# Residual additions made by accumulating transfers from DRAM instead of a loaded tile and a VectorE add

## The chip, the cores and the metric

The kernel runs on one core of a Trainium2 chip. That core has five engines with queues of their own: TensorE (PE in the profile, its weight loads PEld), VectorE (DVE), ScalarE (ACT), GpSimd (POOL) and SyncE (SP), which here only issues transfers. The metric is the device time of one execution in microseconds (us), lower is better. The median of three runs of the kernel before is 2145.02 us (2145.0 to 2145.69).

## The reference

One step of a two-layer encoder, for a prompt of 1024 rows and a running stream of 32 rows that share the weights. The model dimension is 1024. Cut to what matters:

```python
for i in range(DEPTH):                       # DEPTH = 2
    mod = jax.nn.silu(c) @ w_ada[i] + b_ada[i]
    sh1, sc1, gt1, sh2, sc2, gt2 = jnp.split(mod[:, None, :], N_MOD, axis=-1)
    h = rmsnorm(x, g_norm[i, 0]) * (1 + sc1) + sh1
    if i % N_MIXERS == 0:
        mix, v = sgu_mixer(h, ...)           # gated MLP over chunks of 128 rows
    else:
        mix = pool_mixer(h_ext, ...)         # trailing means of 2, 4, 8, 16 rows
    x = x + gt1 * rmsnorm(mix, g_norm[i, 1])
    h = rmsnorm(x, g_norm[i, 2]) * (1 + sc2) + sh2
    f = jnp.square(jax.nn.relu(h @ ffn_w_up[i])) @ ffn_w_down[i]
    x = x + gt2 * rmsnorm(f, g_norm[i, 3])
```

The two lines `x = x + gt * rmsnorm(...)` are the residual additions that this change is about.

## The kernel before, in words

**Tiles.** Activations stand transposed: 128 partitions times 8 blocks `k` of channels, with rows of the batch along the free dimension. There are three tiles of columns (line 27): 384, 384, and 256 prompt rows plus the 32 rows of the stream, 288 in all. For each tile `t` there is one accumulator `acc[t]` in SBUF (128 x 8 x columns, with 16 columns of halo) in which down products are summed and into which norms and modulation are written in place. Since the accumulator is overwritten, the residual stream `x` itself is kept in DRAM, in `xd[t]`.

**Precision.** Every weight and activation is split into a high part (ScalarE, line 436 and others) and a low part (VectorE, a subtraction recorded at line 80), and three matmuls make one product (lines 946 to 948).

**Stages.** First the adaLN vectors of layer 0 and the gate inputs, then six passes of the sgu mixer (`pu` up, `psp` gating, `po` down), then the feed-forward passes of layer 0 (`pf` up, `pg` down), the pooling mixer of layer 1 (`pp`), the feed-forward of layer 1, and the output. Feed-forward passes are cut by chunk of hidden channels and by tile, ordered so that one tile's norms and mixers run beside another tile's matmuls; in a middle stretch two tiles are combined with sums of columns (`sums_of_columns`, line 1782, whose inputs come over DRAM from `md[t]`).

**Work between the matmuls.** What is not a matmul of the main stream is written as Python generators, *fillers*. `weave` (line 744) is called after each block of products: it takes steps of the weight stream (load, split) and of the fillers as long as a model of the two clocks, `time["pe"]` and `time["dve"]`, says that VectorE has room. A filler that yields True goes on at once, False lets others pass, and a number makes it wait that many modelled us. `finish` forces a filler to its end. The tile framework then sets the order of each engine's queue from this, and places the waits. Each engine runs its own queue strictly in order.

**Buffers.** Up products take 2 banks of PSUM, down products 3 (`ps_dn`, line 159), others 3. Raw weights have 3 buffers (`RAW_SLOTS`), split weights 16. Three small buffers `x3` (`t_x`, line 174) are shared by the loaded residual tiles, the gating inputs, the pooling windows and others.

**The residual.** `residual` (line 852) is used eleven times: after the mixer (`r1`) and after the feed-forward (`r2`), for three tiles in two layers, save the last tile's last one, which ends the kernel in another way. It finishes the norm of `acc[t]` (a matmul with ones gives the sums over channels, `pn`, line 839), then loads `xd[t]` in four pieces of two channel blocks into `x3` buffers (line 859, names `xo`), multiplies each block in place by the gate and the norm (`stt`, line 80 in the profile), adds the loaded piece (`tt`, line 882, recorded at line 80), lets ScalarE square the result and VectorE sum the squares (`Stat.square`, line 788, names `sq_..x`), and stores the new `x` from `acc[t]` to `xd[t]` on SP's queue (line 887). In nine of the eleven the squares follow, for the next norm. In the two of the output (`r2_1`) neither squares nor store follow, but transposes by VectorE (line 2118) and stores of the output, a quarter of which POOL issues (line 2120).

SP issues almost all transfers, weights included, in one queue. POOL issues few: some vectors at the start, memsets for the gating inputs (line 1411) and a quarter of the output stores.

Of the kernel before, what the change touches and what calls it, by code (L numbers as in the profile page):

```python
# [12 lines left out]
ALU = mybir.AluOpType  # L13
AX = mybir.AxisListType

P = 128
# [7 lines left out]
HALO = 16  # L24
# [2 lines left out]
TILES = [(0, 384, 0), (384, 384, 0), (768, 256, DEC)]  # L27
NT = len(TILES)
W_SLOTS = 16
COMBINED = [range(2, 6), range(4, 8)]  # L30
RAW_SLOTS = 3
WINDOWS = (2, 4, 8, 16)
# [3 lines left out]
def tile_stream_encoder_step(  # L36
# [25 lines left out]
    nc = tc.nc  # L62
# [11 lines left out]
    def on_dve(op, fixed, rate):  # L74
        def run(out, *args, **kw):
            n = 1
            for k in out.shape[1:]:
                n *= k
            time["dve"] += fixed + n / rate
            return op(out, *args, **kw)  # L80

        return run

    tt = on_dve(nc.vector.tensor_tensor, 0.16, 930.0)
    stt = on_dve(nc.vector.scalar_tensor_tensor, 0.16, 840.0)
    ts = on_dve(nc.vector.tensor_scalar, 0.1, 930.0)

    def pool(name, **kw):
# [10 lines left out]
    segs = [  # L99
        [(0, p, 0)] + ([(p, s, 1)] if s else []) for _, p, s in TILES  # L100
    ]
# [16 lines left out]
    acc = [const.tile([P, KB, HALO + n], F32, name=f"acc{t}") for t, n in enumerate(ncol)]  # L118
    xd = [dram.tile([P, KB, n], F32, name=f"xd{t}") for t, n in enumerate(ncol)]
# [16 lines left out]
        out=squares, in0=ident[:, 0:DEC], in1=ident[:, DEC : 2 * DEC], op=ALU.add  # L136
    )
    for i in (2, 3):
        nc.vector.tensor_tensor(
            out=squares, in0=squares, in1=ident[:, i * DEC : (i + 1) * DEC], op=ALU.add  # L140
# [7 lines left out]
    def A(t, kb, c0=0, w=None):  # L148
        w = ncol[t] - c0 if w is None else w
        return acc[t][:, kb, HALO + c0 : HALO + c0 + w]  # L150
# [23 lines left out]
    def t_x(name, shape):  # L174
        return small.tile(shape, F32, tag="x3", bufs=3, name=name)
# [28 lines left out]
    coef = small.tile([P, 2, 4, NV, KB], F32, name="coef")  # L204
# [118 lines left out]
    runs = []  # L323
    for l, cs in enumerate(COMBINED):
        before = [[(l, c, [0]) for c in (6, 7)] + [(l, 0, pair), (l, 1, [0]), (l, 1, [1])]]
# [83 lines left out]
    def issue():  # L409
        while state["issued"] < len(stream):  # L410
# [9 lines left out]
            else:  # L420
                r = work.tile([P, 1024], F32, tag="W", bufs=W_SLOTS, name=f"raw{k}")
            if kind == "x":
# [10 lines left out]
    def do_w(key, r):  # L433
        wh = work.tile([P, 1024], F32R, tag="W", bufs=W_SLOTS, name="wh_" + "_".join(map(str, key)))
        wl = work.tile([P, 1024], F32R, tag="W", bufs=W_SLOTS, name="wl_" + "_".join(map(str, key)))
        act(out=wh, in_=r, func=AF.Copy)  # L436
        witem[key] = (wh, wl)
        tt(out=wl, in0=r, in1=wh.bitcast(F32), op=ALU.subtract)
# [3 lines left out]
    def cost(key):  # L442
        return 2 if len(key) != 4 or key[0] != "up" else 4 - key[3]
# [14 lines left out]
    def do_s(key, r):  # L458
        p, i, q = key[1:]
        a, b, sh, sl = (  # L460
            work.tile([P, 1024], F32R, tag="W", bufs=W_SLOTS, name=f"{x}_up_{p}_{i}_{q}")
            if q == 0 or x != "wl"
# [174 lines left out]
    def stream_ready():  # L637
# [3 lines left out]
        if stream[k][0] in "ws":  # L641
# [3 lines left out]
            if i < wtight[0]:  # L645
                return i < W_SLOTS // 2 or worder[i - W_SLOTS // 2] in wdone
            used = sum(cost(key) for key in worder[:i] if key not in wdone)
            return used + cost(worder[i]) <= W_SLOTS - max(
                n for n, first in zip([0] + w_taken, [0] + wtight) if i >= first
# [202 lines left out]
    def residual(st, l, cf, tag, out, store=True, stat=True):  # L852
        t = st.t
        n = ncol[t]
        xos = {}

        def load(k2):
            xos[k2] = t_x(f"xo_{tag}_{k2}", [P, 2, n])
            nc.sync.dma_start(xos[k2], xd[t][:, 2 * k2 : 2 * k2 + 2, :])

        got = []
        yield from st.finish(got)
        r = got[0]
        st2 = Stat(t, tag + "x")
        for half in range(2):
            for k2 in (2 * half, 2 * half + 1):
                load(k2)
            for k2 in (2 * half, 2 * half + 1):
                for k in (2 * k2, 2 * k2 + 1):
                    for c0, w, v in segs[t]:  # L870
                        a = A(t, k, c0, w)
                        stt(
                            out=a,
                            in0=a,
                            scalar=coef[:, l, cf, v, k : k + 1],
                            in1=r[:, c0 : c0 + w],
                            op0=ALU.mult,
                            op1=ALU.mult,
                        )
                    yield True  # L880
                a = acc[t][:, 2 * k2 : 2 * k2 + 2, HALO:]
                tt(out=a, in0=a, in1=xos[k2], op=ALU.add)
                if stat:
                    st2.square(2 * k2, a)
                yield k2 % 2 == 0
        if store:
            nc.sync.dma_start(xd[t], acc[t][:, :, HALO:])
        out.append(st2)
# [399 lines left out]
    for half in range(2):  # L1288
# [3 lines left out]
        ks = slice(4 * half, 4 * half + 4)  # L1292
# [454 lines left out]
    def mix_to_ffn(st, l):  # L1747
        t = st.t
        out = []
        need_ada(l, 2)  # L1750
        yield from residual(st, l, 1, f"r1_{l}_{t}", out)
        if l == 1 and t == NT - 1:
            for q in range(P // DEC):
# [140 lines left out]
    def to_pool(st):  # L1894
# [4 lines left out]
        def run():  # L1899
            need_ada(0, 5)  # L1900
            out = []
            yield from residual(st, 0, 3, f"r2_0_{t}", out)
            need_ada(1, 1)
            got = []
# [152 lines left out]
    def to_out(st):  # L2057
# [48 lines left out]
        def run():  # L2106
            need_ada(1, 5)
            if t == NT - 1:
                yield from last()
                return  # L2110
            yield from residual(st, 1, 3, f"r2_1_{t}", [], store=False, stat=False)
            turned = room("h", t, f"turned{t}")
            dst = y_prompt[0, col0 : col0 + npr, :].rearrange(
                "(b i) (k q c) -> q k i b c", i=DEC, q=P // DEC, c=DEC
            )
            for k in range(KB):
                time["dve"] += 0.1 + npr / 930.0
                nc.vector.transpose(out=turned[:, k, :], in_=A(t, k))
                for q in range(P // DEC):
                    (nc.gpsimd if q == 3 else nc.sync).dma_start(  # L2120
                        dst[q, k],
                        turned[DEC * q : DEC * (q + 1), k, :].rearrange("p (b c) -> p b c", c=DEC),
                    )
                yield 5.0
# [50 lines left out]
```

## Time and profile before

| | |
|---|---|
| median of three runs | 2145.02 us |
| the profiled execution | 2145.2 us |
| its span, first to last instruction | 2143.4 us |
| TensorE busy | 2120.2 us (99%) |
| VectorE busy | 1533.1 us (72%) |
| ScalarE busy | 1011.7 us (47%) |
| POOL busy | 15.3 us (1%) |
| mean granted TensorE clock | 0.999 |
| moved by transfers | 321.88 MB, mean 150 GB/s |

The profile is of one execution. Busy time of TensorE includes matmuls that overlap; the groups of instructions give a mean duration per matmul of about 0.32 us, while one starts every 0.17 us. A row of waits tells which engine and line stood idle, and whose end released it. A helper hides the line: nearly all VectorE operations are recorded at line 80, so tiles tell them apart. Landing is the time from a transfer's issue to the semaphore that tells of its end.

### The profile page before, as it was taken

The numbers are of one execution on the slowest core, as the hardware profiler recorded it, in microseconds if no ns is written. First come the engines' busy times: TensorE is split into PE (matmuls) and PEld (weight loads), VectorE is DVE, ScalarE is ACT, GpSimd is POOL, SyncE is SP. The second block draws the span as 40 slices with busy tenths as digits, with TensorE's granted clock in tenths as the row PEclk, the third lists the DMA queues.
The fourth block names the chain that finished last, engine by engine and source line by source line (L and its number), as shares of the span: only waits on it lengthen the run. The fifth ranks groups of instructions, "written<-read, shape, count | busy, mean of one in ns | idle before, by whom it ended". The sixth has DMA issues, their size and how long they took to land.

```text
span 2143.4 us, 33175 instructions
## 1 busy us (share of the span) xinstructions
PE 2120.2 (99%) x13041; PEld 2043.8 (95%) x13041; DVE 1533.1 (72%) x2786; ACT 1011.7 (47%) x1772; POOL 15.3 (1%) x34
## 2 busy tenths in 40 slices
PE   9999999999999999999999999999999999999998
PEld 6778999999999999999999999999999999999998
DVE  6787747466878668897778778969578654578464
ACT  5534322233456255244545556665355443365454
POOL 0000000000000000000000000000000000001000
PEclk9999999999999999999999999999999999999999
DMA  8487524353537454343434576665265322158662
GB/s 309 147 264 211 167 85 128 93 156 103 171 98 239 129 157 131 109 128 118 157 110 132 162 213 201 194 189 169 85 192 156 99 70 59 55 160 232 149 202 77
DMA packets 366002, 321.88 MB, mean 150 GB/s; under 512 B 39731, under 2 KB 328027, under 8 KB 365845
## 3 DMA queue, kind: packets, MB, share of 16 engines
q1 hardware_dynamic: 365172, 318.87, 48.8%
q8 instruction: 102, 1.67, 0.3%
q0 software_dynamic: 640, 0.88, 0.1%
q14 instruction: 56, 0.45, 0.1%
q10 hardware_dynamic: 32, 0.01, 0.0%
HBM read 279.22 MB, written 40.49 MB: 149 GB/s over the span
## 4 chain that ended last, share of the span: by engine, by line
PE 87%; DVE 5%; DMA 5%; ACT 2%; issue 1%; SPq 0%; DVEq 0%; ACTq 0%
PE pg L947 10%; PE pg L946 10%; PE pg L948 10%; PE pf L946 6%; PE pf L947 6%; PE pf L948 6%; PE pf_0a L1610 3%; PE po L947 3%; PE po L946 3%; PE po L948 3%; PE pu L946 3%; PE pu L948 3%; PE pu L947 3%; PE pv L974 2%; PE pv L973 2%; PE pv L975 2%
## 5 line engine op out<-in xcount | busy, mean ns | idle before, releaser
L946 PE MATMUL pg<-fh,wh_dn 128*128 128x384 f32 (+1 forms) x1344 | 431.6, 322 | 1.3 <-ACT fh L1359 1.1
L947 PE MATMUL pg<-fl,wh_dn 128*128 128x384 f32 (+1 forms) x1344 | 428.5, 319 | 0.9 <-DVE fl L80 0.9
L948 PE MATMUL pg<-fh,wl_dn 128*128 128x384 f32 (+1 forms) x1344 | 428.2, 319 | 0.0
L946 PE MATMUL pf<-hh,wh_up 128*128 128x288 f32 (+1 forms) x1024 | 323.2, 316 | 3.8 <-ACT wh_up L436 2.6
L947 PE MATMUL pf<-hl,wh_up 128*128 128x288 f32 (+1 forms) x1024 | 321.9, 315 | 0.8 <-DVE hl L80 0.8
L948 PE MATMUL pf<-hh,wl_up 128*128 128x288 f32 (+1 forms) x1024 | 322.1, 315 | 0.0
L946 PEld LDWEIGHTS pg<-fh,wh_dn 128*128 128x128 f32 x1344 | 252.1, 188 | 5.0 <-ACT fh L1359 3.4
L947 PEld LDWEIGHTS pg<-fl,wh_dn 128*128 128x128 f32 x1344 | 252.2, 188 | 2.2 <-DVE fl L80 1.1
L948 PEld LDWEIGHTS pg<-fh,wl_dn 128*128 128x128 f32 x1344 | 252.2, 188 | 0.0
L80 DVE TENSOR_TENSOR acc<-acc,pg 128x384 f32<-128x384 f32 (+1 forms) x336 | 172.4, 517 | 86.2 <-PE pg L948 85.3
L80 DVE TENSOR_TENSOR wl_dn<-raw,wh_dn 128x1024 fp32r<-128x1024 f32 x144 | 175.8, 1221 | 64.9 <-ACT wh_dn L436 60.3
L80 DVE TENSOR_TENSOR wl_up<-raw,wh_up 128x1024 fp32r<-128x1024 f32 (+1 forms) x160 | 160.3, 1008 | 77.6 <-ACT wh_up L436 66.3
L80 DVE SCALAR_TENSOR_TENSOR aa<-raw,csil,aa 128x512 f32<-128x512 f32 (+1 forms) x364 | 205.8, 624 | 11.6 <-DMA raw<-in_w_ada_dram 11.5
L436 ACT ACTIVATE wh_dn<-raw 128x1024 fp32r<-128x1024 f32 x144 | 151.4, 1055 | 96.8 <-PE pg L947 48.3
L946 PEld LDWEIGHTS pf<-hh,wh_up 128*128 128x128 f32 x1024 | 192.0, 188 | 5.0 <-ACT wh_up L436 3.1
L947 PEld LDWEIGHTS pf<-hl,wh_up 128*128 128x128 f32 x1024 | 192.2, 188 | 1.3 <-DVE hl L80 1.0
L948 PEld LDWEIGHTS pf<-hh,wl_up 128*128 128x128 f32 x1024 | 192.5, 188 | 0.3 <-DVE wl_up L80 0.2
L436 ACT ACTIVATE wh_up<-raw 128x1024 fp32r<-128x1024 f32 x112 | 118.3, 1058 | 134.9 <-PE pf L947 80.3
L946 PE MATMUL pu<-hh,wh_u 128*128 128x384 f32 (+1 forms) x384 | 125.8, 328 | 0.0
L946 PE MATMUL po<-ush,wh_o 128*128 128x384 f32 (+1 forms) x384 | 123.6, 322 | 0.0
L948 PE MATMUL pu<-hh,wl_u 128*128 128x384 f32 (+1 forms) x384 | 123.4, 321 | 0.0
L947 PE MATMUL pu<-hl,wh_u 128*128 128x384 f32 (+1 forms) x384 | 123.3, 321 | 0.0
(453 smaller groups left out, 4130.5 us busy)
## 6 DMA issues: line engine op xcount, KB each, us to landing
raw<-in_ffn_w_up_dram SPq DMA_DIRECT2D x144, 512.0 KB, 4.4
raw<-in_ffn_w_down_dram SPq DMA_DIRECT2D x144, 512.0 KB, 3.6
raw<-in_w_ada_dram SPq DMA_DIRECT2D x96, 512.0 KB, 4.7
raw<-in_sgu_w_in_dram SPq DMA_DIRECT2D x40, 512.0 KB, 4.2
xd<-acc SPq DMA_DIRECT2D x8, 1536.0 KB, 7.6
raw<-in_sgu_w_out_dram SPq DMA_DIRECT2D x24, 512.0 KB, 3.9
xo_r<-xd SPq DMA_DIRECT2D x32, 384.0 KB, 3.4
vd<-vt SPq DMA_DIRECT2D x32, 256.0 KB, 4.4
```

Source lines behind the costliest of these rows:

```text
L80: return op(out, *args, **kw)
L436: act(out=wh, in_=r, func=AF.Copy)
L946: mm(ps[:, :n], wh, rh, start=i == 0, stop=False)
L947: mm(ps[:, :n], wh, rl, start=False, stop=False)
L948: mm(ps[:, :n], wl, rh, start=False, stop=i == last)
L973: mm(ps[:m, :], a_h, wh[:, o : o + 512], start=k == 0, stop=False)
L974: mm(ps[:m, :], a_h, wl[:, o : o + 512], start=False, stop=False)
L975: mm(ps[:m, :], a_l, wh[:, o : o + 512], start=False, stop=k == KB - 1)
L1610: mm(ps[:, :n], u, v, start=first and k == 0 and x == 0, stop=k == 3 and x == 2, skip_group_check=True,)
```

## The change

The load of `xd[t]` into a tile and the VectorE addition are taken out. Instead all blocks of a half are scaled, and then two transfers, issued by POOL, add `xd[t]` from DRAM onto `acc[t]` in SBUF (`accum_op`). The squares are no longer taken block by block behind each addition, but after all four transfers, behind a modelled wait of `ADDED` = 4.0 us. The store of the new `x` on SP's queue follows the squares in the program.

```diff
+ADDED = 4.0
...
     def residual(st, l, cf, tag, out, store=True, stat=True):
         t = st.t
         n = ncol[t]
-        xos = {}
-
-        def load(k2):
-            xos[k2] = t_x(f"xo_{tag}_{k2}", [P, 2, n])
-            nc.sync.dma_start(xos[k2], xd[t][:, 2 * k2 : 2 * k2 + 2, :])
-
         got = []
         yield from st.finish(got)
         r = got[0]
         st2 = Stat(t, tag + "x")
         for half in range(2):
-            for k2 in (2 * half, 2 * half + 1):
-                load(k2)
-            for k2 in (2 * half, 2 * half + 1):
-                for k in (2 * k2, 2 * k2 + 1):
-                    for c0, w, v in segs[t]:
-                        a = A(t, k, c0, w)
-                        stt(
-                            out=a,
-                            in0=a,
-                            scalar=coef[:, l, cf, v, k : k + 1],
-                            in1=r[:, c0 : c0 + w],
-                            op0=ALU.mult,
-                            op1=ALU.mult,
-                        )
-                    yield True
-                a = acc[t][:, 2 * k2 : 2 * k2 + 2, HALO:]
-                tt(out=a, in0=a, in1=xos[k2], op=ALU.add)
-                if stat:
-                    st2.square(2 * k2, a)
-                yield k2 % 2 == 0
+            for k in range(4 * half, 4 * half + 4):
+                for c0, w, v in segs[t]:
+                    a = A(t, k, c0, w)
+                    stt(
+                        out=a,
+                        in0=a,
+                        scalar=coef[:, l, cf, v, k : k + 1],
+                        in1=r[:, c0 : c0 + w],
+                        op0=ALU.mult,
+                        op1=ALU.mult,
+                    )
+                yield k % 2 == 0
+            for k in (4 * half, 4 * half + 2):
+                ks = slice(k, k + 2)
+                nc.gpsimd.dma_start(
+                    out=acc[t][:, ks, HALO:], in_=xd[t][:, ks, :], accum_op=ALU.add
+                )
+        if stat:
+            yield ADDED
+            for k2 in range(4):
+                st2.square(2 * k2, acc[t][:, 2 * k2 : 2 * k2 + 2, HALO:])
                 yield k2 % 2 == 0
         if store:
             nc.sync.dma_start(xd[t], acc[t][:, :, HALO:])
```

Because the modelled VectorE time and the dependencies change, the order of several queues changes with it. Lines of the changed kernel are one higher near the top and three lower below the edit. Three places follow; the numbers at the ends of names count buffers.

VectorE's queue in the first residual of tile 0 (`r1_0_0`), before. `acc0` with `coef` is a scaling, `xo` the addition, `sq` a sum of squares, `po` the accumulation of another tile's down products:

```order
L80 TENSOR_SCALAR acc0_72<-acc0_72,coef_123,r_rs_0_5007 128x384 x3
L80 TENSOR_TENSOR acc0_72<-acc0_72,xo_r1_0_0_0_5054 128x2x384
L80 TENSOR_TENSOR acc1_73<-acc1_73,po4_1_1_5078 128x384
L80 TENSOR_SCALAR acc0_72<-acc0_72,coef_123,r_rs_0_5007 128x384
L80 TENSOR_TENSOR acc1_73<-acc1_73,po4_1_2_5095 128x384
L80 TENSOR_TENSOR acc0_72<-acc0_72,xo_r1_0_0_1_5056 128x2x384
L80 TENSOR_SCALAR acc0_72<-acc0_72,coef_123,r_rs_0_5007 128x384 x2
L80 TENSOR_TENSOR acc1_73<-acc1_73,po4_1_3_5115 128x384
L80 TENSOR_TENSOR acc0_72<-acc0_72,xo_r1_0_0_2_5109 128x2x384
L80 TENSOR_TENSOR sq_r1_0_0x_5075<-sq_r1_0_0x_5075 128x768
```

The same place in the changed kernel:

```order
L81 TENSOR_SCALAR acc0_72<-acc0_72,coef_123,r_rs_0_5007 128x384 x4
L81 TENSOR_TENSOR acc1_73<-acc1_73,po4_1_1_5072 128x384
L81 TENSOR_SCALAR acc0_72<-acc0_72,coef_123,r_rs_0_5007 128x384 x3
L81 TENSOR_TENSOR acc1_73<-acc1_73,po4_1_2_5091 128x384
L81 TENSOR_SCALAR acc0_72<-acc0_72,coef_123,r_rs_0_5007 128x384
L81 TENSOR_TENSOR acc1_73<-acc1_73,po4_1_3_5108 128x384
L81 TENSOR_TENSOR sq_r1_0_0x_5136<-sq_r1_0_0x_5136 128x768
L81 TENSOR_TENSOR acc1_73<-acc1_73,po4_1_4_5122 128x384
L81 TENSOR_TENSOR sq_r1_0_0x_5136<-sq_r1_0_0x_5136 128x768
L81 TENSOR_TENSOR acc1_73<-acc1_73,po4_1_5_5149 128x384
L81 TENSOR_TENSOR sq_r1_0_0x_5136<-sq_r1_0_0x_5136 128x768
```

The additions are gone, the scalings close up, and the sums of squares follow the last scaling with one or two accumulations between.

SP's queue where the last tile's residual of layer 1 ends, before (`raw` are weight loads, `md2<-acc2` the store from which the sums of columns begin, `acc2<-md` and `sums_m` their loads):

```order
L428 DMA raw346_15737<-in_ffn_w_up_dram 128x8x128
L428 DMA raw347_15782<-in_ffn_w_down_dram 128x4x256
L428 DMA raw348_15826<-in_ffn_w_down_dram 128x4x256
L1823 DMA sums_m0_15905<-md1_80 128x384
L1823 DMA sums_m1_15989<-md1_80 128x384
L1774 DMA md2_81<-acc2_74 1024x1x288
L428 DMA raw349_15872<-in_ffn_w_down_dram 128x4x256
L428 DMA raw350_15927<-in_ffn_w_down_dram 128x4x256
L1819 DMA acc2_74<-md1_80 128x384
```

And in the changed kernel:

```order
L429 DMA raw342_15472<-in_ffn_w_down_dram 128x4x256
L429 DMA raw343_15518<-in_ffn_w_up_dram 128x8x128
L1820 DMA sums_m0_15557<-md1_80 128x384
L1820 DMA sums_m1_15641<-md1_80 128x384
L1771 DMA md2_81<-acc2_74 1024x1x288
L429 DMA raw344_15579<-in_ffn_w_up_dram 128x8x128
L429 DMA raw345_15625<-in_ffn_w_up_dram 128x8x128
L1816 DMA acc2_74<-md1_80 128x384
```

The store moved from behind weight load 348 to behind weight load 343, five loads earlier.

POOL's queue from the gating of the fifth group on, before:

```order
L1411 MEMSET vl4_2_5010 128x256
L1411 MEMSET vl5_2_5256 128x256
L1411 MEMSET vl6_2_5708 128x256
L1411 MEMSET vl7_2_5939 128x256
L2120 DMA out_0_dram<-turned0_19127 32x12x32 x8
```

And in the changed kernel:

```order
L1408 MEMSET vl4_2_5010 128x256
L1408 MEMSET vl5_2_5256 128x256
L875 DMA acc0_72<-xd0_75 128x2x384 x4
L1408 MEMSET vl6_2_5700 128x256
L1408 MEMSET vl7_2_5931 128x256
L875 DMA acc1_73<-xd1_76 128x2x384 x4
L875 DMA acc2_74<-xd2_77 128x2x288 x4
```

Four transfers stand in POOL's queue for each residual, the first four ahead of the last two memsets.

## The prediction

> **What bounds the kernel now.** I read the page's first part, then TensorE's waits, then the stretches in which the eleven residual additions run, then the transfers.
>
> ```profile
> span 2143.4 us, 33175 instructions
> ...
> PE 2120.2 (99%) x13041; PEld 2043.8 (95%) x13041; DVE 1533.1 (72%) x2786; ACT 1011.7 (47%) x1772; POOL 15.3 (1%) x34
> ```
>
> The span holds 2120.2 us of busy TensorE, so 23.2 us is all that anything outside TensorE could give. Not all of it is near the change; the waits say who ends the idle time:
>
> ```profile
> PE pf L946 <- ACT wh_up L436: 2.6, 2, 2.0
> PE pv L974 <- DVE wl_v L80: 1.7, 1, 1.7
> PE pn_rf L839 <- ACT sc_rf L824: 1.5, 1, 1.5
> ...
> PE pg L947 <- DVE fl L80: 0.9, 1, 0.9
> ...
> PE pf L947 <- DVE hl L80: 0.8, 1, 0.8
> ```
>
> No row names the residual addition or its loaded tile. Next, the residual stretches (columns: stretch, length, then busy time of PE, PEld, DVE, ACT, POOL with counts, granted clock, DMA share, GB/s), first narrow, then wider ones:
>
> ```profile
> 1200.00:1226.00 26.00, 26.00 (x199) 26.00 (x198) 25.08 (x39) 16.14 (x26) 0.00 (x0) 1.00 0.66 207
> 1318.00:1343.00 25.00, 25.00 (x191) 25.00 (x190) 24.60 (x38) 16.01 (x24) 0.00 (x0) 1.00 0.69 211
> ```
>
> ```profile
> 1195.00:1270.00 75.00, 72.24 (x530) 71.05 (x530) 64.39 (x98) 43.15 (x71) 0.00 (x0) 1.00 0.67 207
> ...
> 1550.00:1630.00 80.00, 78.98 (x453) 78.09 (x452) 58.03 (x108) 45.75 (x78) 0.00 (x0) 1.00 0.62 188
> 1915.00:1980.00 65.00, 62.69 (x457) 62.11 (x456) 60.91 (x106) 36.14 (x62) 9.95 (x16) 1.00 0.78 211
> ```
>
> Inside a residual VectorE is nearly full (25.08 of 26.00 us), yet TensorE never stops there. It stops a little later: 75.00 - 72.24 = 2.76 us in 1195 to 1270, 1.02 us in 1550 to 1630, 2.31 us in 1915 to 1980. The whole prize near the change is thus about 6 us, 0.3% of the time, and any loss must come from new waits.
>
> **What is removed.**
>
> ```profile
> L859 SPq DMA_DIRECT2D xo_r<-xd x44: 319/339/2374, 512.6 to 1959.3; - x44
> L80 DVE TENSOR_TENSOR acc<-acc,xo_r x44: 751/952/968, 530.7 to 1966.6; 128x768 f32<-128x768 f32 x32, 128x576 f32<-128x576 f32 x12
> ```
>
> 44 additions leave VectorE: 32 x 0.952 + 12 x 0.751 = 39.5 us of its 1533.1. None of it is on TensorE's path by itself; it counts where VectorE's backlog later holds TensorE up. There is one clear such place, after the second residual of layer 1's first tile:
>
> ```profile
> L80 DVE TENSOR_TENSOR acc<-acc,xo_r 128x768 f32<-128x768 f32 x4 | 3.8, 952 | 0.0
> ```
>
> ```profile
> 1239.82 1.23 DVE sums L566
> 1241.07 5.38 DMA raw<-in_ffn_w_up_dram
> 1246.47 1.07 ACT wh_up L436
> ...
> 1261.65 1.07 ACT wh_up L436
> 1262.76 0.40 PE pf L946
> ```
>
> The first row is VectorE's work in 1195 to 1270, the second view the chain there (start, length, what). VectorE ends its adaLN sums late, which frees a raw buffer late, so a weight load starts late and TensorE waits for wh_up: the 2.6 us above. Four additions, 3.8 us, stand ahead of those sums. If VectorE ran 3.8 us earlier all 2.6 us would go; if it spends the saving waiting for squares, nothing goes. Bounds 0 and -2.6; I take the middle, **-1.3**, because the new waits fall on the same queue.
>
> Second place: the wait of 0.9 us for fl. Its chain:
>
> ```profile
> 1594.99 5.79 DMA md<-acc
> ...
> 1623.60 0.56 DVE fl L80
> 1624.21 0.44 PE pg L947
> ```
>
> It starts at the store md<-acc that ends the last tile's residual of layer 1. In the changed order this store stands five weight loads earlier in SP's queue (shown ahead of this section). Bounds 0 and -0.9; I take **-0.9**. The waits of 1.5 and 0.8 us lie in 1915 to 1980, where the additions (the last starts at 1966.6) mostly follow them: 0, with -1.5 as the bound.
>
> SP loses 44 issues. It does wait in them, but far longer for the weights' raw buffers:
>
> ```profile
> SPq L428 <- DVE wl_dn L80: 372.5, 110, 12.9
> ...
> SPq L859 <- DVE acc L80: 46.3, 18, 9.6
> ```
>
> A raw buffer freed by VectorE, not SP's place in line, dates the weight loads. I cost this at 0 beside the 2.6 us already counted. In return the store of the residual on SP now waits for the fourth landing instead of an addition, with weight loads queued behind it; three raw buffers in flight and the converted weights cover that as long as it is a few us.
>
> **What is added.** 44 transfers issued by POOL, and behind them ScalarE's squares, then VectorE's sums of squares, both in order with work for TensorE. The trace shows no accumulating transfer; the nearest rows are these:
>
> ```profile
> xd<-acc SPq DMA_DIRECT2D x8, 1536.0 KB, 7.6
> ...
> xo_r<-xd SPq DMA_DIRECT2D x32, 384.0 KB, 3.4
> ```
>
> ```profile
> L2120 POOL DMA_DIRECT2D out_dram<-turned x16: 615/617/653, 1942.6 to 1976.5; - x16
> ```
>
> POOL's own time is 44 x 0.617 = 27 us on an engine busy 15.3 us: nothing waits for that in itself. One memset of the gating stands behind the first four issues in POOL's queue; before, it waited for the third addition of that same residual, so it comes hardly later. Landing: a plain load of the same bytes lands 3.4 us after a 0.339 us issue, so from POOL 3.4 + 0.617 - 0.339 = 3.7 us. From 384 to 1536 KB landing grows by 4.2 us, so 1.4 us for each further 384 KB and 2.0 us fixed. If the addition makes the engines handle every byte twice, one takes 2.0 + 0.3 + 2.8 = 5.1 us, and four in a row need 2.8 us each.
>
> How long may it take? In the changed order the eighth scaling stands ahead of VectorE's fourth po accumulation and the sum that needs the fourth square behind the sixth: two blocks of twelve matmuls.
>
> ```profile
> 837.05 2.08 PE pf_0b L1610 x12
> ```
>
> ```profile
> L794 ACT ACTIVATE sq_r_0x<-acc x12: 827/847/850, 531.7 to 1221.6; 128x768 f32<-128x768 f32 x12
> ```
>
> ```profile
> L80 DVE TENSOR_TENSOR acc<-acc,pg 128x384 f32<-128x384 f32 (+1 forms) x336 | 172.4, 517 | 86.2 <-PE pg L948 85.3
> ```
>
> Two blocks are 4.2 us; less the square of 0.85 the landing may take 3.3 us before ScalarE and VectorE stand still. TensorE stops later still: of three banks for down products it can fill two more, 2 x 2.08 less the 0.52 us accumulation = 3.6 us. So:
> - landing of 3.7 us: 0.4 us late, covered: 0 lost;
> - every byte twice: issues for a whole residual spread over about 4.2 us, the fourth lands 5.1 + 3 x 2.8 = 13.5 us after the first issue, 9.3 us after its own, 6.0 us late: 2.4 us lost.
>
> Nine residuals take squares (the two of the output do not; their transposes follow directly, and there VectorE waits as long at most). Ends: 0 and 9 x 2.4 = 22 us. The 384 KB load is the nearest row, since bytes, layout and direction are the same, so I stay near the low end, 0.5 us each, **+4.5**: the transfer engines are already 0.66 to 0.69 busy there with weights; against that, three of the nine residuals are a quarter smaller (128x576). If that cover is gone (lateness above 3.6 us) each us more costs nine.
>
> How the engines treat an addition decides between the ends. The Trainium skill, page "Collectives: The Full Stack", section "The bandwidth ceiling: the fold count and why AG ≠ RS ≠ AR", says that an adding transfer is slowed by its two source reads and not by the add, 62.28 against 32.35 GB/s. By it the sum would use the second case, +22 in place of +4.5; no row here has such a transfer, so nothing tests it yet.
>
> **Sum.** -1.3 - 0.9 + 4.5 = +2.3 us. The profiled execution took 2145.2 us (span 2143.4 and 1.8 around it), 0.2 above the runs' median of 2145.02: 2145.2 + 2.3 - 0.2 = **2147.3 us**. A measurement of this kernel tells about 0.2% from no change, 4.3 us, so this is no change.
>
> **Rivals.**
> - *The landings hold up ScalarE and VectorE* (slower). Place: squares of the nine residuals. Price: up to 2.4 us each, 2145.0 - 2.2 + 22 = 2165 us; it decides from 0.75 us each (4.3 + 2.2 over nine), a fourth landing some 7.7 us after its issue. For it: DMA share 0.66 to 0.69 in the stretches and a byte handled twice, the mechanism to which the page's rule leads. Against: the store row, which moves four times the bytes in 7.6 us; and VectorE gets 3.8 us back in each residual to spend on waiting.
> - *VectorE's relief shows, landings stay hidden* (faster). Then the waits of 2.6, 0.9 and 1.5 us go: 2145.0 - 5.0 = 2140 us. For it: VectorE is full in every residual stretch, and the change empties it just there. Against: those waits also hang on loads of 4 to 5 us, and all three must go to pass 4.3 us.
> - That the additions are not moved at all cannot be: the order has no xo tile left and four POOL transfers per residual.
>
> **Chances.** Forecast (2141 to 2149.3) 0.48, slower rival 0.35, faster rival 0.17. The range 2140 to 2162 leaves out about 0.08 of the faster and 0.10 of the slower rival.
>
> **What would show it.** Right: no acc<-acc,xo_r rows, VectorE busy near 1533.1 - 39.5 = 1494 us; POOL-issued transfers landing in 4 to 6 us; idle time of the squares ended by the DMA, some us per residual, but TensorE's own waits still under 30 us in all and no new row above 2 us; the waits for wh_up and fl smaller. Wrong: landings of 8 us or more, TensorE waiting for fh, acc or wh_up beside each residual (slower), or all three old waits gone with no new one (faster). What I could miss most is queueing: weights and four adding transfers at once on engines two thirds busy.

## The result, and the profile after

The changed kernel takes 2311.15 us (median; 2306.5 to 2313.5) beside 2145.36 us of the kernel before on the same chip: a ratio of 1.077, 95% interval 1.0751 to 1.0789. The change costs 166 us. The forecast was 2147.3 us and no change. It was wrong: even its slower rival was priced at 2165 us.

The profiled execution took 2312.9 us. From its page, the span and the busy times:

```profile
span 2311.1 us, 33201 instructions
...
PE 2158.9 (93%) x13041; PEld 2071.3 (90%) x13041; DVE 1503.7 (65%) x2742; ACT 1012.3 (44%) x1772; POOL 68.7 (3%) x78
```

VectorE lost the additions as intended: 2786 - 2742 = 44 instructions and 29.4 us of busy time (39.5 were forecast; the removed durations do add up to that, but the records of neighbouring operations overlap, and busy time counts an overlap once). TensorE idles 2311.1 - 2158.9 = 152.2 us, where it idled 23.2 before: 129.0 us more. The same 13041 matmuls are also busy 2158.9 - 2120.2 = 38.7 us longer. Together that is the 167.7 us between the two spans. The second part goes with the granted clock, whose mean fell from 0.999 to 0.968.

The stretches with TensorE's busy time, clock, DMA share and GB/s place the loss. First a stretch of the kernel before, in which TensorE never stops:

```profile
500.00:730.00 230.00, 230.00 (x1454) 1.00 0.52 159
```

Then the changed kernel. Its first and third stretch hold residuals, the second holds none:

```profile
500.00:730.00 230.00, 196.62 (x1196) 0.92 0.49 131
730.00:1130.00 400.00, 397.13 (x2287) 1.00 0.41 127
1130.00:1430.00 300.00, 254.51 (x1651) 0.92 0.54 148
```

TensorE's waits name the engines that ScalarE's squares and VectorE's sums block:

```profile
PE pf L943 <- ACT r L1531: 51.7, 9, 13.1
PE pg L943 <- ACT fh L1356: 25.5, 7, 9.4
PE pf L945 <- DVE wl_up L81: 17.1, 2, 15.4
PE pn_r_0x L840 <- ACT sc_r_0x L825: 10.5, 1, 10.5
```

The cause is one view further down. These are the 44 transfers themselves: the duration of an issue on POOL, what ended POOL's idle time ahead of one, who waited, and the landing:

```profile
L875 POOL DMA_DIRECT2D acc<-xd x44: 1189/1207/1261, 530.7 to 2121.3; - x44
...
  issue: 218.5, 25
...
  ACT sq_r_0x L795: 57.9, 12
  ACT sq_r_2x L795: 53.2, 11
  ACT sq_r_1x L795: 47.1, 12
...
DMA to landing us min/median/max: 4.6/5.5/8.2
```

An issue takes 1.207 us, and 25 times POOL stands idle ahead of one with nothing that the profile shows to wait for ("issue"). One of these waits, 102.4 us ahead of the first transfer of a residual, is only the time between two residuals; the other 24 are 116.1 us, 3.9 to 7.3 us each. In order of time, the first residual on POOL and ScalarE (start, length, idle time before and its releaser):

```profile
530.70 1.26 POOL L875 DMA_DIRECT2D acc<-xd  x1 [17.61 <-DVE acc L81]
536.47 1.23 POOL L875 DMA_DIRECT2D acc<-xd  x1 [4.51 <-issue]
541.98 1.21 POOL L875 DMA_DIRECT2D acc<-xd  x1 [4.28 <-issue]
547.73 1.21 POOL L875 DMA_DIRECT2D acc<-xd  x1 [4.54 <-issue]
```

```profile
536.29 0.85 ACT L795 ACTIVATE sq_r_0x<-acc 128x768 f32<-128x768 f32 x1 [7.59 <-DMA acc<-xd]
...
553.42 0.84 ACT L795 ACTIVATE sq_r_0x<-acc 128x768 f32<-128x768 f32 x1 [5.15 <-DMA acc<-xd]
```

Each transfer is issued only when the one before has landed: the first square starts at 536.29, POOL's next issue at 536.47. The fourth piece lands 22.7 us after the first issue (553.42 - 530.70). In the kernel before, the fourth square of this residual started at 540.14:

```profile
531.70 0.85 ACT L794 ACTIVATE sq_r_0x<-acc 128x768 f32<-128x768 f32 x1 [3.12 <-DVE acc L80]
...
540.14 0.85 ACT L794 ACTIVATE sq_r_0x<-acc 128x768 f32<-128x768 f32 x1 [2.88 <-DVE acc L80]
```

One residual thus ends 13.3 us later, and there are eleven, nine of them with squares.

### The profile page after: what moved, and what is told of

Same layout as the page of the kernel before. It is cut to its first block, busy times and chain, and to the rows that moved or that the text cites. A ratio compares the mean times of both kernels' runs of the same rounds, so it can differ in the third digit from the quotient of the medians.

```text
span 2311.1 us, 33201 instructions
## 1 busy us (share of the span) xinstructions
PE 2158.9 (93%) x13041; PEld 2071.3 (90%) x13041; DVE 1503.7 (65%) x2742; ACT 1012.3 (44%) x1772; POOL 68.7 (3%) x78
## 3 DMA queue, kind: packets, MB, share of 16 engines
q0 software_dynamic: 12608, 17.01, 5.0%
## 5 line engine op out<-in xcount | busy, mean ns | idle before, releaser
L943 PE MATMUL pg<-fh,wh_dn 128*128 128x384 f32 (+1 forms) x1344 | 438.9, 327 | 38.5 <-ACT fh L1356 25.5
L944 PE MATMUL pg<-fl,wh_dn 128*128 128x384 f32 (+1 forms) x1344 | 435.6, 324 | 6.0 <-DVE fl L81 5.8
L945 PE MATMUL pg<-fh,wl_dn 128*128 128x384 f32 (+1 forms) x1344 | 433.7, 323 | 0.0
L943 PE MATMUL pf<-hh,wh_up 128*128 128x288 f32 (+1 forms) x1024 | 328.5, 321 | 53.9 <-ACT r L1531 51.7
L945 PE MATMUL pf<-hh,wl_up 128*128 128x288 f32 (+1 forms) x1024 | 327.1, 320 | 17.1 <-DVE wl_up L81 17.1
L943 PEld LDWEIGHTS pg<-fh,wh_dn 128*128 128x128 f32 x1344 | 256.9, 191 | 45.2 <-ACT fh L1356 28.6
L944 PEld LDWEIGHTS pg<-fl,wh_dn 128*128 128x128 f32 x1344 | 257.2, 191 | 10.2 <-DVE fl L81 8.9
L945 PEld LDWEIGHTS pg<-fh,wl_dn 128*128 128x128 f32 x1344 | 257.2, 191 | 0.2 <-DVE wl_dn L81 0.2
L944 PE MATMUL po<-usl,wh_o 128*128 128x384 f32 (+1 forms) x384 | 124.0, 323 | 0.0
L945 PE MATMUL po<-ush,wl_o 128*128 128x384 f32 (+1 forms) x384 | 123.9, 323 | 0.0
```

Source lines behind the costliest of these rows:

```text
L943: mm(ps[:, :n], wh, rh, start=i == 0, stop=False)
L944: mm(ps[:, :n], wh, rl, start=False, stop=False)
L945: mm(ps[:, :n], wl, rh, start=False, stop=i == last)
```

## The experiments

The program has no wait between the transfers, so there are two explanations of the single file. *Room*: a transfer under way takes up part of a memory for descriptors (the entries that say which pieces to move), whose size the kernel sets (`dynamic_dma_scratch_size`, 1024 bytes a partition here), and that holds one such transfer. *One at a time*: accumulating transfers follow one another whatever the memory. All times are medians, each beside the kernel before in the same session (2147.74, 2148.42 and 2145.91 us in the three sessions; where that matters, a difference between sessions is taken from the ratios).

**A little more room.**

```diff
-        "TRN2", target_bir_lowering=False, num_devices=1, dynamic_dma_scratch_size=1024
+        "TRN2", target_bir_lowering=False, num_devices=1, dynamic_dma_scratch_size=1088
```

> The changed kernel with one number changed: the memory kept in SBUF for the descriptors of POOL's transfers is 1088 bytes a partition instead of 1024. Theory 1, room: POOL issues the next accumulating transfer only when the memory for the descriptors has room, and 1024 bytes hold one transfer of 384 KB but not two; if the small step is enough for a second one, the issues come in pairs 1.2 us apart (now 5.5 to 5.8 us apart), the fourth lands some 12 to 14 us after the first issue instead of 22 to 23, and the time falls to 2200 to 2260 us; if it is not enough, nothing changes, which leaves theory 1 open. Theory 2, one at a time: accumulating transfers follow one another whatever the memory, spacing 5.5 to 5.8 us, time 2305 to 2315 us.

Measured: 2244.01 us, ratio 1.0456 (1.0439 to 1.0474). POOL in the first residual, then ScalarE's fourth square there:

```profile
533.03 2.52 POOL L875 DMA_DIRECT2D acc<-xd  x2 [17.61 <-DVE acc L81]
538.54 1.21 POOL L875 DMA_DIRECT2D acc<-xd  x1 [2.99 <-issue]
541.41 1.21 POOL L875 DMA_DIRECT2D acc<-xd  x1 [1.66 <-issue]
```

```profile
547.07 0.84 ACT L795 ACTIVATE sq_r_0x<-acc 128x768 f32<-128x768 f32 x1 [2.19 <-DMA acc<-xd]
```

Two are now issued back to back, the third when the first has landed, and the fourth piece is there 14.0 us after the first issue. 64 bytes a partition are worth 67 us. *One at a time* falls, and that the number of bytes changes the spacing is what *room* says. Two transfers do not fit in 1024 bytes and do in 1088, so if they take equal shares, one takes more than 512 and at most 544 bytes a partition.

**Room for all four.** The bytes are paid for by one raw weight slot, so a control has two slots and the old memory.

```diff
-RAW_SLOTS = 3
+RAW_SLOTS = 2
...
-        "TRN2", target_bir_lowering=False, num_devices=1, dynamic_dma_scratch_size=1024
+        "TRN2", target_bir_lowering=False, num_devices=1, dynamic_dma_scratch_size=4096
```

> The changed kernel with 4096 bytes a partition for the descriptors of POOL's transfers, paid for by one raw weight slot less (two instead of three). Theory 1, room: all four transfers of a residual are issued about 1.2 us apart; each then lands in 5.5 us or somewhat more since they share the engines, the fourth 9 to 13 us after the first issue; the residuals' part of the loss falls by more than half, time 2170 to 2220 us plus whatever the missing raw slot costs. Theory 2, one at a time: spacing stays 5.5 to 5.8 us and the time is 2311 us or more.

The control, without the last line:

> The changed kernel with two raw weight slots instead of three and the descriptor memory as it was (1024 bytes): the control for the run with 4096 bytes, 2263.8 us. If the larger descriptor memory alone did what that run showed, this one is slower than it by about what four transfers at once are worth, 70 to 110 us: 2330 to 2375 us. If the missing slot had nothing to do with the rest, it is near 2311 us, and the larger memory is worth some 47 us.

Measured: 2263.81 us (ratio 1.0534) with room, 2360.17 us (1.0981) in the control. With room, POOL and ScalarE in the first residual:

```profile
545.27 3.77 POOL L875 DMA_DIRECT2D acc<-xd  x3 [17.60 <-DVE acc L81]
549.37 1.19 POOL L875 DMA_DIRECT2D acc<-xd  x1 [0.33 <-DVE acc L81]
```

```profile
550.49 0.85 ACT L795 ACTIVATE sq_r_0x<-acc 128x768 f32<-128x768 f32 x1 [7.22 <-DMA acc<-xd]
553.17 0.85 ACT L795 ACTIVATE sq_r_0x<-acc 128x768 f32<-128x768 f32 x1 [1.83 <-DMA acc<-xd]
555.64 0.85 ACT L795 ACTIVATE sq_r_0x<-acc 128x768 f32<-128x768 f32 x1 [1.62 <-DMA acc<-xd]
557.75 0.84 ACT L795 ACTIVATE sq_r_0x<-acc 128x768 f32<-128x768 f32 x1 [1.26 <-DMA acc<-xd]
```

POOL waits for room no longer, and the memory alone is worth 96 us beside the control, as *room* expected (70 to 110). The missing slot costs 1.0981 - 1.0770 in the ratios, 45 us; with it the expected 2170 to 2220 becomes 2215 to 2265 us, which just holds the measured time. Without it the four transfers at once would leave some 70 us of the loss (an estimate: 1.0534 less 0.0211). What is left is the landings: with all four under way they come 2.7, 2.5 and 2.1 us apart, the fourth 12.5 us after the first issue.

**Half as large, twice as many.**

```diff
-            for k in (4 * half, 4 * half + 2):
-                ks = slice(k, k + 2)
+            for k in range(4 * half, 4 * half + 4):
+                ks = slice(k, k + 1)
```

> The changed kernel with eight transfers of one block (192 KB) for a residual instead of four of two blocks. Theory 1, room: half as many descriptors each, so that at least two are under way together: issues about 1.2 us apart in pairs or more, the eighth lands no later than the fourth did, 16 to 23 us after the first issue, and the first block of all lands earlier; time 2250 to 2310 us. Theory 2, one at a time: eight landings of some 4 to 5 us follow one another, 32 to 40 us for a residual, and the time rises to 2380 to 2480 us.

Measured: 2247.55 us, 64 us better than four larger ones, with the same bytes and the old memory, and a little better than expected from *room*. The issue of half the rows takes 875 ns instead of 1207:

```profile
L875 POOL DMA_DIRECT2D acc<-xd x88: 856/875/1582, 529.8 to 2056.9; - x88
...
  issue: 23.0, 18
```

POOL's waits without a shown cause fell from 116.1 us (without the one between residuals) to 23.0 us.

**The same transfer without the addition.**

```diff
-            nc.sync.dma_start(xos[k2], xd[t][:, 2 * k2 : 2 * k2 + 2, :])
+            nc.gpsimd.dma_start(xos[k2], xd[t][:, 2 * k2 : 2 * k2 + 2, :])
```

> The kernel before with one word changed: the four loads of x of each residual are issued by POOL instead of SP, plain copies into a tile, and VectorE adds as before. It tells the price of POOL's issue from that of the accumulation. If what costs is any transfer of 384 KB from POOL's queue, the issues are 4 to 6 us apart here too and the time is 2200 us or more. If it is the accumulation, the loads are issued about 1.2 us apart, land in 3.4 to 4.5 us, hidden behind the DVE work as SP's are, and the time is 2140 to 2155 us.

Measured: 2146.19 us, ratio 0.9997 (0.9987 to 1.0006). Plain loads from POOL:

```profile
L859 POOL DMA_DIRECT2D xo_r<-xd x44: 538/538/585, 513.4 to 1963.5; - x44
...
DMA to landing us min/median/max: 3.0/3.6/6.9
```

POOL's queue is not the cost; the accumulating transfer is. For the same bytes its issue takes 1207 instead of 538 ns and its landing 5.5 instead of 3.6 us. Two things differ, the addition and the destination: `acc` has 16 columns of halo between its blocks, the tile `xo` has no gaps (the run with a spare tile, below, separates them). The packets of POOL's queue (packets, MB, share) suggest why the memory fills; the rows are of the kernel before, this run, the changed kernel and the run with half-size transfers:

```profile
q0 software_dynamic: 640, 0.88, 0.1%
```

```profile
q0 software_dynamic: 4160, 17.01, 2.8%
```

```profile
q0 software_dynamic: 12608, 17.01, 5.0%
```

```profile
q0 software_dynamic: 13312, 17.01, 5.0%
```

A plain transfer makes (4160 - 640)/44 = 80 packets, an accumulating one (12608 - 640)/44 = 272, half of one (13312 - 640)/88 = 144. If room goes by packets, 513 to 544 bytes for 272 are 1.9 to 2.0 bytes each (an estimate), and of the half-size transfers three fit into 1024 bytes and a fourth does not. In the first residual of that run three are issued back to back from 529.83 to 532.57, and the fourth, whose block was scaled by 531.1, only at 534.05.

**Nothing added at all.** Two runs price VectorE's relief, one in the new order and one in the old.

```diff
-            for k in (4 * half, 4 * half + 2):
-                ks = slice(k, k + 2)
-                nc.gpsimd.dma_start(
-                    out=acc[t][:, ks, HALO:], in_=xd[t][:, ks, :], accum_op=ALU.add
-                )
```

> The changed kernel with the 44 accumulating transfers left out: x is not added at all, so the sums are not the reference's; everything else, the order of the squares included, stays. Theory 1, the transfers are the loss: ScalarE's squares wait for nothing long, the loss goes, and the time is 2135 to 2150 us; the distance to 2147.7 is all that the removed VectorE additions and loads are worth. Theory 2, the new order is the loss (all squares of a tile after all its products, in one block at the end): the time stays above 2170 us.

```diff
-            for k2 in (2 * half, 2 * half + 1):
-                load(k2)
...
-                tt(out=a, in0=a, in1=xos[k2], op=ALU.add)
```

> The kernel before with the 44 additions and their 44 loads left out, all else in its old order; x is not added, so the result is another. It prices the relief that the prediction put at 2.2 us. If the predicted gain terms are right: 2145 to 2147 us beside 2148 us of the kernel before, ratio 0.998 to 0.9995. If VectorE's relief is worth the full stalls near the residuals: 2141 to 2143 us. If it is worth nothing: within 0.05% of the kernel before, and the 2151.6 us of the new order without transfers then show a price of the order.

Measured: 2151.64 us in the new order, ratio 1.0013 (1.0004 to 1.0022); 2148.25 us in the old, ratio 1.0016 (1.0007 to 1.0025). Both are slower than any gain that was expected: with no addition at all the kernel is not faster. They lie 3.2 and 2.3 us above the kernel before, with intervals that overlap, so the new order by itself costs next to nothing, and taking the additions and their loads away is worth nothing here. Why is seen in the old-order run at the place where the prediction had booked its largest gain:

```profile
PE pf L945 <- DVE wl_up L80: 2.4, 1, 2.4
```

The 2.6 us of waiting for wh_up were two waits, the longer of 2.0 us; here stands one of 2.4 us for wl_up, with 0.5 us of others. The clock in the same place (stretch, length, TensorE busy, clock, DMA share, GB/s), first in the kernel before, then in this run:

```profile
1262.00:1264.00 2.00, 1.24 (x9) 1.00 0.62 183
1264.00:1266.00 2.00, 2.00 (x17) 1.00 0.76 203
```

```profile
1264.00:1266.00 2.00, 0.11 (x1) 1.00 0.46 112
1266.00:1268.00 2.00, 1.45 (x6) 0.60 0.60 174
1268.00:1270.00 2.00, 2.00 (x11) 0.55 0.97 268
```

Before, the clock stayed at 1.00 through the pause, of which the end is shown. Here it fell, and for some 4 us TensorE did 11 matmuls in 2 us instead of 17.

**Transfers for which nobody waits.**

```diff
-                nc.gpsimd.dma_start(
-                    out=acc[t][:, ks, HALO:], in_=xd[t][:, ks, :], accum_op=ALU.add
-                )
+                e = t_x(f"e_{tag}_{k}", [P, 2, n])
+                nc.gpsimd.memset(e, 0.0)
+                nc.gpsimd.dma_start(out=e, in_=xd[t][:, ks, :], accum_op=ALU.add)
```

> The changed kernel, its transfers still accumulating and its descriptor memory still 1024 bytes, but adding x onto a spare tile that POOL has cleared and nobody reads; x is so left out of the result. POOL's issues, the 44 serial landings and their traffic stay, and only the waits of the squares, the transposes and the store for a landing go. Theory 1, waiting for landings is the whole loss: 2148 to 2156 us, as with the transfers left out (2151.6 us), with POOL's spacing still 5 to 6 us. Theory 2, the transfers disturb others by themselves (weights arrive later, engines slower): a good part of the 160 us stays, over 2180 us.

Measured: 2178.41 us, between the two expectations: by the ratios, 133 us below the changed kernel and 30 above the run without transfers. The 30 us come at least in part from the edit: its spare tiles are buffers that other loads use too, and SP and TensorE stand at those:

```profile
SPq L1909 <- DMA e_r<-xd: 24.4, 1, 24.4
```

```profile
PE pp L2026 <- DMA wg<-in_pool_w_grp_dram: 14.0, 1, 14.0
```

The spare tile has no gaps, and its transfers are lighter (issue, then packets, then landing):

```profile
L877 POOL DMA_DIRECT2D e_r<-xd x44: 857/872/1249, 513.1 to 1929.5; - x44
```

```profile
q0 software_dynamic: 6976, 17.01, 4.7%
```

```profile
e_r<-xd POOLq DMA_DIRECT2D x32, 384.0 KB, 5.4
```

That is (6976 - 640)/44 = 144 packets. So the addition alone, onto a tile without gaps like the plain load's, raises 80 packets to 144, 538 ns to 872 and a landing of 3.6 us to 5.4. The gaps of `acc` raise the packets further to 272 and the issue to 1207 ns, and leave the landing at 5.5 us. (No run makes a plain load into a tile with gaps.)

The edit thus changes more than the waits: half the packets, and issues that no longer wait for scalings (the first at 513.1 instead of 530.7). Their spacing is set by the memsets ahead of them, which wait for an earlier transfer (104.6 us in 28 waits), and at times two are issued together. About 133 of the 166 us go with the waits for landings and with these differences; of the other 33 this run cannot tell how much is the transfers' own traffic.

**Squares held back.** What remains once two fit (96 us in the run with 1088 bytes) could be squares that stand too early in ScalarE's queue.

```diff
-ADDED = 4.0
+ADDED = 12.0
...
-        "TRN2", target_bir_lowering=False, num_devices=1, dynamic_dma_scratch_size=1024
+        "TRN2", target_bir_lowering=False, num_devices=1, dynamic_dma_scratch_size=1088
```

> The run with 1088 bytes for descriptors, and ADDED 12.0 instead of 4.0, so that the squares stand 8 modelled us of other work later in ScalarE's and VectorE's queues. Theory 1, head of the queue: what is left of the loss there (96 us) is ScalarE standing at a square whose piece has not landed, with evictions behind it; the waits of the three sq groups for the transfer, 94 us in all there, fall below 35 us and the time to 2165 to 2205 us. Theory 2, the chain: the next norm needs the squares anyway, so holding them back only moves the wait to TensorE's next products; the time stays within 10 us of 2244 us or rises.

And with the old memory, `ADDED = 24.0`:

> The changed kernel with ADDED 24.0 instead of 4.0 and the descriptor memory as it was (1024 bytes): the transfers stay one at a time, the fourth landing 22 to 23 us after the first issue, but the squares stand 20 modelled us later. Theory 1, head of the queue: ScalarE's 158 us of waits for the transfers fall below 60 us and the time to 2190 to 2250 us. Theory 2, the chain: what ScalarE no longer waits, TensorE waits for the next norm; the time stays 2290 to 2340 us.

Measured: 2222.95 us and 2311.83 us. ScalarE's waits for the transfers at the squares, over all three groups, are 90.7 us beside 94, and 161.4 beside 158.2: they hardly moved. Between the first issue and the first square ScalarE does no more than 5 instructions in the first run and 2 in the second, as before the edit (0 to 5). The number did not bring the squares behind other work. So neither run tests the head of the queue as meant, and that the second stayed at the old time is no evidence for the chain. The 21 us of the first were not traced to a cause.

**A mixed version.** One pair of each residual accumulates, scaled first and squared last; the others are loaded and added as before.

```diff
...
+        for k in (6, 7):
+            scale(k)
+            yield True
+        nc.gpsimd.dma_start(
+            out=acc[t][:, 6:8, HALO:], in_=xd[t][:, 6:8, :], accum_op=ALU.add
+        )
+        for half in ((0, 1), (2,)):
...
+        if stat:
+            st2.square(6, acc[t][:, 6:8, HALO:])
```

> A mixed version: of each residual one pair of blocks, scaled first and squared last, is added by an accumulating transfer (11 in all, never two at once), the other three by loads and VectorE as before. Between the issue and the last square lie six scalings and three additions of VectorE, some 6 us, against a landing of 5.5 us. Theory 1, only uncovered landings cost: the loss nearly goes, 2146 to 2156 us. Theory 2, each accumulating transfer costs by itself: a quarter of the 163 us, 2180 to 2195 us. A gain over the kernel before is not expected from either, since leaving the additions out altogether gave none in the new order.

Measured: 2158.57 us, ratio 1.0062 (1.005 to 1.0075), just above the first expectation's range and far from the second's. Landings without cover are what costs, and even this cover does not always reach:

```profile
ACT sq_r_2x L794 <- DMA acc<-xd: 11.7, 3, 6.4
```

No version with accumulating transfers beat the kernel before, and the runs without any addition say that there was nothing to win.

## Why the prediction was wrong

**The bound and the prize: right, and still too high.** TensorE was the bound, and the stalls near the residuals were 6 us at most. The gain terms, -1.3 and -0.9 us, were wrong in sign: without additions and loads the time rose by 2.3 us in the old order. The largest stall kept its place under another name, and the 2.6 us booked for it were two waits, of which only the one of 2.0 us stands at the place that was shown. With that the faster rival has no ground either.

**POOL's issue, the step that failed.** The prediction priced an issue at 0.617 us from the output stores, 27 us in all, with the sentence "nothing waits for that in itself". An issue took 1.207 us; that alone would have been harmless. What failed is that the issues were taken to be independent: "issues for a whole residual spread over about 4.2 us". They were 5.5 to 5.8 us apart in the first residual, and in none less than 5.06, because POOL waited for room. The row used could not show that: the stores have 48 KB each. The number 1024 stands in the lines that launch the kernel and was not weighed.

**The landing: its size right, its use wrong.** "Every byte twice" gave 5.1 us alone and 2.8 us for each further one; measured were 5.5 us, and 2.1 to 2.7 us in series once there was room for four. For the fourth, 13.5 us after the first issue was worked out; with room it was 12.5 us, without 22.7. Choosing the plain load as "nearest row" (0.5 us lost each) was the wrong end: bytes and direction were the same, but that row has no addition, and its layout was not the same either, since `acc` has gaps. The case "every byte twice" was the right one for the landing. The Trainium skill, page "Collectives: The Full Stack", section "The bandwidth ceiling: the fold count and why AG ≠ RS ≠ AR", tells of collectives that two source reads slow an adding transfer. The traces agree for a transfer of one core: without gaps 144 packets against 80, and 5.4 us to land against 3.6.

**The cover, the second step that failed.** Even with room for two the loss was 96 us, and with room for four some 70 (the estimate above), where the prediction's upper case gave 22. It allowed 3.3 us before ScalarE stands still and 3.6 us of TensorE's banks behind that, both read from one place in the order. In the trace ScalarE has at most 5 instructions (2.8 us) between a first issue and its square, and in three of the nine residuals none. It then stands 7.6 us ahead of a first square (536.29), with evictions behind it.

**The slower rival** had the right place and mechanism, squares that hold up ScalarE and VectorE. Its price of 2.4 us each came from a fourth landing 9.3 us after its own issue and a cover that is not there. The sentence "If that cover is gone (lateness above 3.6 us) each us more costs nine" was the warning: the fourth came 22.7 us after the first issue, 9.2 later than in that case.

**What was left out** is the clock: 38.7 of the 167.7 us are longer busy time of the same matmuls, which goes with a lower clock after pauses, a cost that no term had.

**What would show it:** VectorE was to be near 1494 us and was at 1503.7; no new wait of TensorE above 2 us, and there are waits of 13.1 and 15.4; landings of 4 to 6 us, and 5.5 was measured, so that sign alone would have misled. "What I could miss most is queueing" was right, but the queue was POOL's memory, not the engines.

## What to carry to other kernels

Before a transfer is moved to another queue or made to add, ask how many of it can be under way at once, what holds its descriptors, and whether its destination stands in separate pieces (that nearly doubled the packets here); a row of single landings does not tell. A landing that takes the place of an engine's operation needs work ordered behind it on every engine that waits for it, and that work must be counted in the queue, at each place. An engine that is full beside a bound that never stops is not a cost: leave the work out entirely, once, and see whether the time moves, before buying it off.

## What the runs showed of the hardware

- *An accumulating transfer is another kind of transfer.* 384 KB by POOL onto a tile without gaps: 0.872 against 0.538 us to issue, 5.4 against 3.6 us to land, 144 against 80 packets; onto `acc`, with its gaps, 1.207 us, 5.5 us and 272 packets. With 1024 bytes for descriptors an issue also waited, without a wait that the profile names, until the transfer before had landed; 64 bytes a partition more were worth 67 us.
- *A pause costs more than its length.* In the changed kernel TensorE stood 10.5 us for the first residual's norm (the wait for sc_r_0x above), until 556.5 us, and went on at half the clock (columns as above):

```profile
556.00:558.00 2.00, 1.45 (x5) 0.50 1.05 386
...
560.00:562.00 2.00, 2.00 (x17) 0.96 0.00 0
```

  The clock came back some 3.5 us after work did. The Trainium skill, page "TensorE: Matmul & The Clock Gate", section "Part 1: The HAM clock gate (the "warmup" mystery)", tells of a gate that passes half of the clock after an idle window of about 3.4 us and all of it after a busy one, and that the window runs free. These rows agree with the half and with the return, but shorter pauses than 3.4 us were enough: one of 2.4 us lowered the clock in the run without additions, while the one of about 2 us in the kernel before did not. Nor does the length decide, as two pauses of the changed kernel show (the matmul that ends each, with the pause in brackets, and the clock behind it):

```profile
674.07 0.44 PE L943 MATMUL pf<-hh,wh_up 128*128 128x384 f32 x1 [2.58 <-ACT r L1531]
```

```profile
674.00:676.00 2.00, 1.93 (x11) 1.00 0.91 124
```

```profile
682.16 0.45 PE L943 MATMUL pg<-fh,wh_dn 128*128 128x384 f32 x1 [1.48 <-ACT fh L1356]
```

```profile
684.00:686.00 2.00, 2.00 (x8) 0.50 1.06 376
```

  The pause of 2.58 us left the clock at 1.00, and the one of 1.48 us was followed by 0.50. Where a pause falls, and what idleness went before it, may decide; no run here isolates that.
